# Output projection of a hybrid encoder on 16-bit halves, scaled by per-row powers of two

## The chip, the cores and the metric

The kernel runs on one core of a Trainium2 chip. The metric is the device time of one execution in microseconds (us). Before the change it is 2007.9 us, the median of three runs.

## The reference

One layer of an encoder is applied to two sequences that share weights: a prompt of 1024 rows and a sample of 4096 rows, each row 1024 wide, all in 32-bit floating point.

```python
def hybrid_layer(x, norm_g, w_in, sink, dw_w, dw_b, ln_g, ln_b, w_out):
    h = rms_norm(x, norm_g)
    proj = h @ w_in                       # 1024 -> 2816
    q, k, v, g_attn, u_conv, g_conv = jnp.split(proj, SPLITS, axis=-1)
    attn = windowed_gqa(q, k, v, sink)    # 8 heads of 64, 2 kv heads, |t-s| <= 128
    conv = conformer_conv(u_conv, dw_w, dw_b, ln_g, ln_b)   # GLU, 31 taps, LayerNorm, SiLU
    mix = jnp.concatenate([attn * silu(g_attn), conv * silu(g_conv)], axis=-1)
    return x + mix @ w_out                # 1024 -> 1024
...
y = rms_norm(hybrid_layer(x, ...), final_g)
```

The inputs' gains are scaled up (the LayerNorm's gain and bias by some 35 times, the first norm's gain by 6.8), so the two halves of `mix` reach far beyond what a 16-bit number holds unscaled.

## The kernel before, in words

The 5120 rows make ten groups of 512 rows (two of the prompt, eight of the sample), each of four blocks of 128 rows. A 32-bit operand enters a matmul as two parts, a high one (the value rounded) and a low one (what the rounding left), and a product is three matmuls: high by high, high by low, low by high. The input projection does this with 16-bit parts (`inproj`, L345: 8 slices of 128 rows times 3 pairs, 24 matmuls of 128x128 by 128x512 for each of 22 column tiles). The output projection does it with parts in the 32-bit rounded type (`out_mm`, L763: 8 slices times 3 pairs times 2 halves of 512 columns, 48 matmuls for a block, 1920 in all).

**Stage A** (to about 848 us) goes over the groups with `slot`: attention of one block, preparation of rows of the group after next (`prep_x`: load into a tile `xb`, norm, split, transposition by DMA) and a share of the next group's projection onto k, v, q and the attention gate. After each of the first six groups it also prepares two weight tiles for stage B (`split_late`: load into `xb`, `scale_w` finds a power of two from the largest entry by a reduction on DVE, a transposition and a broadcast on PE, and the parts go back to DRAM; L325 is its subtraction on POOL). At the end of `attention` three instructions form the gated output and its parts (L531 to L533: product on DVE, rounding on ACT, difference on DVE) in the tile `mx`, and a DMA stores the pair in DRAM (`md`, 512 KB).

**Stage B** goes over the groups again. `start_b` loads the group's prepared rows, `glu` projects eight column tiles (L632 on ACT, L633 on DVE free the matmul bank), `gates` projects four more through `conv_gate` (L639, SiLU on ACT into `sgc`, which the trace calls `x` after its tag). `conv_chunk` does the 31 taps on DVE (L695, L697), `ln_batch` and `ln_norm` the LayerNorm, and `ln_act` applies SiLU and gate (L751, L753) and splits into the tile `mc` (L754 on ACT, L755 on DVE). For each block `out_first` loads the rows `x` into `xb` and the attention pair into `ma`, and does the first 24 matmuls; `out_second` does the other 24 with `mc`, adds to the rows (L794 on DVE, two halves), sums the squares (L795 on ACT, writing back into the matmul's bank), finds the norm's factor on POOL in 11 small steps (L797, L260 to L269), scales (L806 on ACT), multiplies by `final_g` (L807 on POOL) and stores. Before the first block `load_out` brings in w_out with `split_wout`: a load into `xb`, for the four attention slices a factor (L335, POOL) and a scaling (L336, ACT), then rounding (L337, ACT) and difference (L338, POOL).

**What sets the order.** Nothing is issued as it is written down. Each operation is put into a plan with its engine and a cost in ns (`pl.op`), and `flush` simulates the engines and writes out every engine's instructions in the order of the simulated starts; of those that could start at the same time the one written first goes first. So a changed cost can change the order of everything near it. Tiles with a tag come from a ring of a fixed number (`xb` 2, matmul banks `mm` 4, `ma` 1, `mc` 2, `xn` 2), handed out in the order in which the code asks. All DMAs go through the queue of SP in the planned order; one that waits for its tile holds up those behind it. There are two flushes, one for each stage.

## Time and profile before

| | |
|---|---|
| runs | 2006.31, 2007.9, 2014.75 us; median 2007.9 |
| the profiled execution | 2009.39 us, its span 2007.5 us |
| mean granted TensorE clock | 0.975 of full speed |
| instructions | 25966 |

The profile is of one execution. Its span runs from the first to the last instruction; the execution is 1.9 us longer. PE is TensorE's matmuls, PEld its weight loads, DVE VectorE, ACT ScalarE, POOL GpSimd, SP SyncE, which only issues DMAs here. A matmul's duration is modelled and overlaps the next one's, so the rate of matmuls is read from the time of a run of them, not from their mean. A row names the line, engine, operation, out<-in and the number of instructions, then busy time, mean ns of one, and the idle time before them with what ended it. "x" before a number counts instructions. In the chain of waits each piece is followed back to what released it.

### The profile page before, as it was taken

The page shows a single profiled execution, that of the slowest core. Times are in us where ns is not written, and L with a number is a line of the kernel's source. Part 1 is how long each engine was busy: PE and PEld are TensorE (multiplying, and loading weights), DVE is VectorE, ACT ScalarE, POOL GpSimd, SP SyncE. Part 2 cuts the span into 40 slices and gives each one's busy share as a digit, 9 for nine tenths or more (in the row PEclk, how much of TensorE's full clock was granted, in tenths as well). Part 3 has the DMA queues.
Part 4 walks back from the last instruction along what each step waited for, and adds up shares of the span by engine and source line. Part 5 has one row for each costly group of instructions (what it writes and reads, how often), then busy time and mean ns, then how long its engine had stood idle before and what let it go on. Part 6 is the DMA issues. An engine that isn't in the chain of part 4 may idle for free. (4 is left out here: it accounts for less than half of the span.)

```text
span 2007.5 us, 25966 instructions
## 1 busy us (share of the span) xinstructions
PE 1868.7 (93%) x8953; PEld 1028.1 (51%) x8953; DVE 1800.7 (90%) x3703; ACT 907.0 (45%) x1962; POOL 663.1 (33%) x902
## 2 busy tenths in 40 slices
PE   3999998999999999987999899999999999999987
PEld 1444443444444444433648455564755657474675
DVE  7687897998998798699999998999999897998996
ACT  3577797797888777631213221221312222131332
POOL 1422233232333000060705508073451606143264
PEclk9999998999999999998999999999999999999988
DMA  7577978998999988641103211121221212132022
GB/s 246 137 151 195 232 188 214 223 201 222 226 206 235 232 215 175 141 147 63 64 21 127 74 53 63 73 74 43 84 84 64 86 73 74 42 105 95 32 95 95
DMA packets 364068, 259.39 MB, mean 129 GB/s; under 512 B 328352, under 2 KB 328480, under 8 KB 361376
## 3 DMA queue, kind: packets, MB, share of 16 engines
q1 hardware_dynamic: 363936, 257.73, 48.1%
q8 instruction: 70, 1.15, 0.2%
q14 instruction: 62, 0.51, 0.1%
HBM read 106.70 MB, written 69.21 MB: 88 GB/s over the span
## 5 line engine op out<-in xcount | busy, mean ns | idle before, releaser
L345 PE MATMUL mm<-x,wA 128*128 128x512 f16 x4800 | 1092.8, 383 | 32.3 <-ACT mm L795 17.4
L697 DVE SCALAR_TENSOR_TENSOR acc<-h,taps,acc 128x512 f32<-128x512 f32 (+2 forms) x1380 | 873.5, 693 | 2.0
L345 PEld LDWEIGHTS <-wA 128*128 128x128 f16 x4800 | 471.5, 99 | 583.6 <-issue 50.9
L763 PE MATMUL mm<-wo,mc 128*128 128x512 f32 x960 | 235.9, 401 | 4.0 <-ACT mc L754 3.9
L763 PE MATMUL mm<-wo,ma 128*128 128x512 f32 x888 | 218.9, 401 | 3.0 <-ACT mm L795 3.0
L493 DVE CUSTOM_DVE_ANT_0 pe<-s,dist_sb,sink_sb 128x384 f32<-128x384 f32 (+1 forms) x320 | 201.2, 658 | 15.1 <-PE s L490 13.3
L509 DVE SCALAR_TENSOR_TENSOR pe<-pe,rc 128x384 f16<-128x384 f32 (+1 forms) x320 | 187.9, 627 | 21.5 <-ACT pe L508 20.4
L763 PEld LDWEIGHTS mm<-wo,mc 128*128 128x128 f32 x960 | 179.9, 190 | 46.8 <-ACT mc L754 4.4
L797 POOL TENSOR_SCALAR v<-ms 128x1 f32<-128x1 f32 x38 | 34.3, 902 | 497.8 <-ACT mm L795 495.4
L763 PEld LDWEIGHTS mm<-wo,ma 128*128 128x128 f32 x888 | 167.8, 190 | 45.3 <-ACT mm L795 3.7
L501 ACT ACTIVATE pe<-pe,nm 128x384 f32<-128x384 f32 (+1 forms) x320 | 188.5, 590 | 3.2 <-DVE nm L493 2.8
L508 ACT ACTIVATE pe<-pe,rc 128x384 f16<-128x384 f32 (+1 forms) x320 | 175.6, 594 | 31.6 <-DVE rc L505 22.6
L807 POOL TENSOR_TENSOR xb<-xb,fg 128x1024 f32<-128x1024 f32 x37 | 129.9, 3511 | 88.7 <-ACT xb L806 88.6
L632 ACT ACTIVATE h<-mm,ucolh 128x512 f32<-128x512 f32 x40 | 27.3, 683 | 218.4 <-PE mm L345 218.4
L345 PE MATMUL mm<-x,xt 128*128 128x512 f16 x480 | 113.4, 395 | 0.0
L806 ACT ACTIVATE xb<-xb,r 128x1024 f32<-128x1024 f32 x37 | 42.4, 1145 | 151.9 <-POOL r L269 151.9
L489 PE MATMUL s<-kst,qst 128*128 128x384 f16 (+1 forms) x320 | 102.1, 321 | 8.9 <-DVE nm L493 6.6
L751 ACT ACTIVATE xn<-c,vec_sb 128x128 f32<-128x128 f32 x160 | 60.1, 456 | 108.6 <-PE c L744 85.7
L490 PE MATMUL s<-kst,qst 128*128 128x384 f16 (+1 forms) x320 | 101.7, 320 | 0.0
L795 ACT ACTIVATE mm<-xb 128x512 f32<-128x512 f32 x70 | 41.2, 589 | 120.5 <-DVE xb L794 120.5
L365 POOL TENSOR_SCALAR msv<-ms 128x1 f32<-128x1 f32 x36 | 8.4, 232 | 240.6 <-ACT xt L364 240.2
L267 POOL TENSOR_SCALAR rs_oa<-rs_oy,v 128x1 f32<-128x1 f32 x76 | 82.0, 1080 | 8.0
(164 smaller groups left out, 1940.0 us busy)
## 6 DMA issues: line engine op xcount, KB each, us to landing
xb<-x_s SPq DMA_DIRECT2D x62, 512.0 KB, 4.1
xd<-x SPq DMA_DIRECT2D x10, 2048.0 KB, 7.5
md<-mx SPq DMA_DIRECT2D x40, 512.0 KB, 3.4
x<-xd SPq DMA_DIRECT2D x10, 2048.0 KB, 7.9
ma<-md SPq DMA_DIRECT2D x37, 512.0 KB, 3.3
y_s<-xb SPq DMA_DIRECT2D x29, 512.0 KB, 2.6
xb<-x_p SPq DMA_DIRECT2D x14, 512.0 KB, 3.4
xb<-w_in SPq DMA_DIRECT2D x12, 512.0 KB, 4.6
```

Source lines behind the costliest of these rows:

```text
L267: pl.op(eng, cost + 80, lambda: en.tensor_scalar(a.t, view(cur), view(cur), v.t, ALU.mult, ALU.mult), [cur, v], [a])
L345: T.matmul(ps.t, w16.t[:, a, k, :], x16.t[:, b, k, :], start=(k == 0 and i == 0), stop=(k == KD - 1 and i == 2))
L489: T.matmul(sv(), q, kst.t[:, 2 * kv, kc0 : kc0 + n], start=True, stop=False)
L490: T.matmul(sv(), q, kst.t[:, 2 * kv + 1, kc0 : kc0 + n], start=False, stop=True)
L493: pl.op("DVE", 198 + n / 0.96, lambda: V.tensor_tensor_reduce(sc_(hh), sv(), dist_b.t[:, kv, d0 : d0 + n], gcol[:, hh : hh + 1], sink_sb[: ...
L501: pl.op("ACT", 280 + 0.834 * n, lambda hh=hh: S.activation(sc_(hh), sc_(hh), AF.Exp, bias=nm.t[:, hh : hh + 1], scale=-1.0, accum_out=den. ...
L508: pl.op("ACT", c_act(n, 1), lambda hh=hh: S.activation(p16(hh, 0), sc_(hh), AF.Copy, scale=rc.t[:, hh : hh + 1]), [rc, (pe, hh + 2)], [(pe ...
L509: pl.op("DVE", c_dve(n, 1), lambda hh=hh: V.scalar_tensor_tensor(p16(hh, 1), sc_(hh), rc.t[:, hh : hh + 1], p16(hh, 0), ALU.mult, ALU.subt ...
L697: pl.op("DVE", c_dve(n, 1), lambda: V.scalar_tensor_tensor(a.t[:, :n], src(), w, a.t[:, :n], ALU.mult, ALU.add), hr + [a], [a])
L751: pl.op("ACT", c_act(128, 2), lambda: S.activation(z.t[:, j, :], bk.t[:, j, :], AF.Silu, bias=vec_sb[:, 2, j : j + 1], scale=vec_sb[:, 1, ...
L763: T.matmul(po[hf].t, m.t[:, a, k - k0, :], wo.t[:, k, b, hf * 512 : (hf + 1) * 512], start=(k == 0 and a == 0 and b == 0), stop=(k == KD - ...
L807: pl.op("POOL", 2700, lambda: GP.tensor_tensor(xb.t, xb.t, fg.t, ALU.mult), [xb, fg], [xb])
```

## The change

The output projection's operands become 16-bit. Each of the 1024 rows of w_out (that is, each channel of `mix`) is multiplied by a power of two, its counterpart on the other side by the inverse, and the sum is scaled back by one common factor.

- `row_scales`, new, after group 6 of stage A: ten small DVE instructions that bound each channel of the convolution half by LayerNorm gain, bias and gate scale (`LNMAX`), take the power of two above it, and give `rsc` (factors for the rows of w_out) and `gsc` (inverse factors for the gates). For the attention half the factor is the one that `split_wout` computed before, with a constant `MSCALE` on the other side.
- `max_wout`, new, four slices after group 6 and four after group 7: loads a slice of w_out into `xb` and reduces it to its largest entry per row on DVE.
- `scale_wout`, new, after group 7: the common power of two, by the pattern of `scale_w` (nine small DVE instructions, a transposition and a broadcast on PE).
- `split_wout`: the factor of POOL goes away; two ACT passes (scale into 16 bit; scale in place) and POOL's difference for all eight slices.
- `attention`: the product has a tile `t2` of its own; the rounding scales by `MSCALE`; the difference is a scalar-tensor-tensor; the stored pair has 256 KB.
- `conv_gate`: a second ACT pass scales the gate by `gsc`, in place.
- `out_mm`: planned at 432 ns for a pair of matmuls, was 466; the matmuls are the same in number and shape.
- `out_second`: the add multiplies the matmul's result by the common factor `inv` (scalar-tensor-tensor).
- `wo`, `ma`, `mc` take half the bytes.

The diff, without the ten lines of `row_scales` and the nine small instructions of `scale_wout`:

```diff
@@ row_scales, max_wout, scale_wout (new) @@
+    def max_wout(k):
+        w = pl.buf(pxA, [P, D], F32, "xb", 2)
+        dma(lambda: w.t, lambda: w_out[:, k, :], 524288, [], [w])
+        pl.op("DVE", 1130, lambda: V.tensor_reduce(wmx_b.t[:, k : k + 1], w.t, AX.X, ALU.max, apply_absolute_value=True), [w], [(wmx_b, k)])
+    def scale_wout():
...
+        pl.op("PE", 110, lambda: T.transpose(pt.t[0:1, 0, :], mr.t[:, 0:1], ident), [mr], [pt])
...
+        pl.op("PE", 230, lambda: T.matmul(pb.t[:, 0, 0:2], ones, e2.t, start=True, stop=True), [e2], [pb])
...
@@ split_wout @@
-        if k < 4:
-            sc = small(smB, 1, "wsc", 2)
-            pl.op("POOL", 340, lambda: GP.tensor_scalar(sc.t, ...), ...)
-            pl.op("ACT", c_act(1024, 1), lambda: S.activation(w.t, w.t, AF.Copy, scale=sc.t), [w, sc], [w])
-        pl.op("ACT", c_act(1024), lambda: S.activation(wo.t[:, k, 0], w.t, AF.Copy), [w], [(wo, k)])
-        pl.op("POOL", 2200, lambda: GP.tensor_tensor(wo.t[:, k, 1], w.t, wo.t[:, k, 0].bitcast(F32), ALU.subtract), [w, (wo, k)], [(wo, k)])
+        sc = lambda: rsc_b.t[:, k : k + 1]
+        pl.op("ACT", c_act(1024, 1), lambda: S.activation(wo.t[:, k, 0], w.t, AF.Copy, scale=sc()), [w, rsc_b], [(wo, k)])
+        pl.op("ACT", c_act(1024, 1), lambda: S.activation(w.t, w.t, AF.Copy, scale=sc()), [w, rsc_b], [w])
+        pl.op("POOL", 2200, lambda: GP.tensor_tensor(wo.t[:, k, 1], w.t, wo.t[:, k, 0], ALU.subtract), [w, (wo, k)], [(wo, k)])
@@ attention @@
-        mx = pl.buf(pat, [P, 2, 4, P], F32R, "mx", 1)
+        t2, mx = pl.buf(pat, [P, 4, P], F32, "t2", 1), pl.buf(pat, [P, 2, 4, P], F16, "mx", 1)
...
+        pl.op("ACT", c_act(512), lambda: S.activation(mx.t[:, 0], t2.t, AF.Copy, scale=MSCALE), [t2], [(mx, 0)])
+        pl.op("DVE", c_dve(512, 1), lambda: V.scalar_tensor_tensor(mx.t[:, 1], t2.t, MSCALE, mx.t[:, 0], ALU.mult, ALU.subtract), [t2, (mx, 0)], [(mx, 1)])
+        md = dbuf([P, 1024], F16, f"md{si}_{ab}")
+        dma(lambda: md.t, lambda: mx.t.rearrange("p a j t -> p (a j t)"), 262144, [mx], [md])
@@ the loop over groups in stage A @@
+        else:
+            if gi == 6:
+                row_scales()
+            for k in range(4 * (gi - 6), min(KD, 4 * (gi - 6) + 4)):
+                max_wout(k)
+            if gi == 7:
+                scale_wout()
@@ conv_gate @@
+        pl.op("ACT", c_act(512, 1), lambda: S.activation(sgc.t[:, i, j, :], sgc.t[:, i, j, :], AF.Copy, scale=gsc_b.t[:, j : j + 1]), [(sgc, (i, j)), gsc_b], [(sgc, (i, j))])
@@ wo, ln_act, out_first: F32R becomes F16; the load of ma has 262144 bytes @@
@@ out_mm @@
-                pl.op("PE", 466, mm, [(m, a) if k0 else m, (wo, k)], po)
+                pl.op("PE", 432, mm, [(m, a) if k0 else m, (wo, k)], po)
@@ out_second @@
-                pl.op("DVE", c_dve(512), lambda: V.tensor_tensor(xs(), xs(), po[hf].t, ALU.add), [po[hf], (xb, hf)], [(xb, hf)])
+                pl.op("DVE", c_dve(512, 1), lambda: V.scalar_tensor_tensor(xs(), po[hf].t, inv_b.t, xs(), ALU.mult, ALU.add), [po[hf], (xb, hf), inv_b], [(xb, hf)])
```

## Rows read from the trace of the kernel before

**Rows 1.** The page's busy time, share of the span and instructions of each engine

```profile
PE 1868.7 (93%) x8953; PEld 1028.1 (51%) x8953; DVE 1800.7 (90%) x3703; ACT 907.0 (45%) x1962; POOL 663.1 (33%) x902
```

**Rows 2.** Busy time by stretch; columns us, busy (x instructions), PEclk, DMA share, GB/s

```profile
600.00:800.00 200.00, 198.87 (x1066) 93.30 (x1064) 171.09 (x448) 154.56 (x376) 19.12 (x55) 1.00 0.92 213
848.00:943.00 95.00, 74.04 (x325) 33.55 (x324) 95.00 (x155) 19.61 (x22) 31.78 (x11) 0.89 0.28 95
943.00:1200.00 257.00, 240.89 (x1080) 147.72 (x1079) 254.36 (x511) 60.97 (x120) 93.43 (x96) 0.96 0.22 76
...
1290.00:1409.60 119.60, 113.02 (x514) 67.97 (x512) 118.13 (x185) 26.58 (x53) 53.37 (x48) 0.97 0.20 71
1409.60:1525.00 115.40, 111.16 (x514) 67.84 (x512) 109.28 (x173) 26.80 (x53) 48.45 (x48) 0.99 0.20 73
1525.00:1640.00 115.00, 113.00 (x514) 67.98 (x513) 104.60 (x165) 26.70 (x53) 41.41 (x48) 0.98 0.21 74
...
1924.00:2007.50 83.50, 66.95 (x277) 52.87 (x277) 67.54 (x207) 27.56 (x59) 41.58 (x60) 0.88 0.26 95
```

**Rows 3.** The chain that ended last: shares by line, then start us, us, what

```profile
by line: DVE acc L697 13.6%; PE mm L763 12.4%; PE mm L345 3.2%; POOL xb L807 1.1%; DVE wA L697 1.1%; DVE bst L712 0.8%; DVE h L633 0.7%; issue 0.7%; PE c L744 0.7%; DVE xb L794 0.5%; DVE acc L695 0.4%; POOL rs_oa L267 0.4%; DMA ma<-md 0.3%;
...
1215.26 16.17 POOL xb L807
...
1539.98 11.20 PE mm L763 x48
...
1580.03 10.39 PE mm L345 x48
```

**Rows 4.** Matmul groups by line; columns as on the page (busy us, mean ns, idle)

```profile
L345 PE MATMUL mm<-x,wA 128*128 128x512 f16 x4800 | 1092.8, 383 | 32.3 <-ACT mm L795 17.4 <-DMA x<-xd 7.9 <-DMA x<-pT 3.0
...
L763 PE MATMUL mm<-wo,mc 128*128 128x512 f32 x960 | 235.9, 401 | 4.0 <-ACT mc L754 3.9
```

**Rows 5.** Groups of DVE, by line

```profile
L794 DVE TENSOR_TENSOR xb<-xb,mm 128x512 f32<-128x512 f32 x76 | 48.6, 681 | 25.1 <-DMA xb<-x_s 24.8 <-issue 0.3
...
L633 DVE SCALAR_TENSOR_TENSOR h<-h,mm 128x512 f32<-128x512 f32 x40 | 27.1, 678 | 13.5 <-ACT h L632 13.5
...
L290 DVE TENSOR_REDUCE w_mx<-xb 128x1 f32<-128x1024 f32 x12 | 14.5, 1208 | 0.0
...
L316 DVE SCALAR_TENSOR_TENSOR wA<-qst,w_sg,wA 128x1024 f16<-128x1024 f32 x3 | 3.8, 1276 | 0.0
...
L283 DVE TENSOR_TENSOR pe<-pe,ng 128x1024 f32<-128x1024 f32 x3 | 3.6, 1216 | 0.0
...
L307 DVE TENSOR_SCALAR w_sg<-s 128x1 f32<-128x1 f32 x19 | 2.9, 154 | 12.6 <-PE s L305 12.3
```

**Rows 6.** Groups of POOL and ACT by line, then DVE's timeline from 849 to 890 us

```profile
L639 ACT ACTIVATE x<-mm,ucol 128x512 f32<-128x512 f32 x40 | 25.9, 683 | 64.5 <-PE mm L345 64.5
L325 POOL TENSOR_TENSOR xt<-xb,xt 128x1024 f16<-128x1024 f32 x12 | 25.5, 2128 | 87.7 <-ACT xt L324 87.7
...
L338 POOL TENSOR_TENSOR wo<-xb,wo 128x1024 fp32r<-128x1024 f32 x8 | 19.5, 2447 | 7.5 <-ACT wo L337 7.5
...
849.26 25.49 DVE L697 SCALAR_TENSOR_TENSOR acc<-h,taps,acc 128x384 f32<-128x384 f32 x48
...
875.26 14.61 DVE L697 SCALAR_TENSOR_TENSOR acc<-h,taps,acc 128x384 f32<-128x384 f32 x12
```

**Rows 7.** DMA issues; KB each, median us from issue to landing

```profile
y_s<-xb SPq DMA_DIRECT2D x29, 512.0 KB, 2.6
...
y_s<-xb SPq DMA_DIRECT2D x2, 256.0 KB, 2.0
```

**Rows 8.** Waits of DVE, PE and SP's queue: us in total, times, longest us

```profile
DVE xb L794 <- DMA xb<-x_s: 24.8, 4, 8.3
...
PE s L305 <- DVE w_e L303: 19.1, 6, 10.8
...
SPq L229 <- POOL xt L325: 31.7, 9, 6.3
```

51 lines of the change are left out of this document (39 added, 12 removed).

## The prediction

> **What bounds the kernel now.** I read the busy shares first: TensorE (PE) 93%, VectorE (DVE) 90%, ScalarE (ACT) 45%, GpSimd (POOL) 33% [rows 1]. Two engines near the top say that the share alone won't decide, so the next view is the table by stretch [rows 2]. The change puts its new work into stage A (attention, up to about 848 us) and takes work out of stage B (convolution and output projection, from there to the end). Three regimes are to be seen there. From 600 to 800 us PE is busy 198.9 of 200 us and DVE 171.1: PE is the limit and DVE has 28.9 us free. From 848 to 1200 us DVE is busy 95.0 of 95 and 254.4 of 257 us: DVE is the limit. The step from 1290 to 1409.6 us is still nearly so (DVE idle 1.5 us, PE 6.6). In the group steps from 1409.6 us on PE is the limit: from 1525 to 1640 us PE is idle 2.0 of 115 us and DVE 10.4. The last 83.5 us are a tail in which neither is full.
>
> Then the chain of waits, whose first long piece starts at 1215 us [rows 3]. It goes to and fro between DVE's convolution (L697) and PE, and the output matmuls (L763) stand on it with 12.4% of the span, 249 us. This is the number that the forecast rests on: matmuls elsewhere lie beside something longer.
>
> **The change part by part.** *Matmuls.* All 1920 output matmuls go from 32-bit rounded to 16-bit operands of the same shape, 128x128 by 128x512; the number stays. The mean durations (401 and 383 ns) [rows 4] overlap and give no rate, so I take it from chain pieces: 48 matmuls of L763 take 11.20 us, 233.3 ns each, and 48 of the 16-bit L345 take 10.39 us, 216.5 ns each [rows 3]. So PE gets 16.8 ns less per matmul, 32.3 us over all 1920. On the chain the 249 us are 1067 matmuls; at 216.5 ns they save 17.9 us. The other 853 lie before 1215 us, where DVE is full, or beside the chain, and I give them nothing. Ends: 0 (DVE or another wait takes it all) and 32.3 us. I take **-17.9**. The cover for it: in a PE-bound step 192 matmuls lose 3.2 us, and DVE has 6.1 us idle in the step from 1409.6 us and 10.4 in that from 1525 us [rows 2]; next late is DVE.
>
> A rule speaks against this term. The Trainium skill (Perfetto Trace Analysis, Identifying the Most-Contended Engine) calls matmul busy time a poor measure of headroom and wants the used share of its peak rate and the busy share of the weight loads instead. The weight loads are busy 68.0 of 115 us in the step from 1525 us [rows 2], so by the rule PE has some 40% to spare and a shorter matmul would save nothing. The chain pieces of back-to-back matmuls decide for me, since there every 48 of them take their 11.20 us.
>
> *DVE, residual add (L794).* Two instructions for each of 40 blocks become a scalar-tensor-tensor with a per-row scalar (76 stand in the row; those of two late blocks write a tile of another name). Lower end 0: such an instruction with a constant, reading PSUM, takes 678 ns (L633) beside 681 for the add now. Upper end: at 1024 columns with a per-row scalar it takes 1276 ns (L316) against 1216 (L283), so 60 ns each, 4.8 us [rows 5]. I take half the upper end, **+2.4**, since DVE is the limit for about half of stage B.
>
> *Preparing the weights.* POOL loses four one-column instructions, and its eight subtractions write 16-bit: 2447 ns (L338) become 2128 (L325, the same shape with 16-bit output), 2.6 us less. POOL is not the limit, but DVE runs slowly beside it: 48 taps took 25.49 us, 0.53 each, and 12 of the same size soon after, beside L338 by the order of the code, 14.61, 1.22 each [rows 6]. DVE is full there, so I count **-2.0**, ends 0 and -2.6. ACT does sixteen 1024-wide passes in place of twelve, each at most twice the 0.68 us of the 512-wide L639, so 5.5 us more; from 848 to 943 us ACT is busy 19.6 of 95 us [rows 2], so nothing. If that cover were gone, 5.5.
>
> *Gate scaling.* 40 more ACT passes of 512 columns, each at most the 683 ns of L639 [rows 6], 27 us; 36 of them in stage B, where ACT is busy 26.7 of 115 us. Behind each on ACT's queue wait the next gate, and the tanh that frees PE's bank; four matmul banks cover 0.7 us. Nothing; uncovered it is 0.7 on each of nine steps, 6 us.
>
> *Pairs through memory.* Store and load of the attention half shrink from 512 to 256 KB. The landing of an output goes from 2.6 to 2.0 us at these sizes [rows 7]. The loads stand on the chain with 0.3% (6 us) [rows 3] in two pieces, so **-1.2**; ends 0 and -6, were they to leave it. Forty stores get as much shorter in stage A, beside PE: nothing. The product, its copy and its residual in stage A stay three instructions of the same sizes.
>
> *Bounds of w_out.* New in stage A: eight loads of 512 KB, eight DVE reductions of 1024 columns at 1208 ns (L290), 19 small DVE instructions at about 154 (L307) [rows 5], 12.6 us in all; one transposition and one broadcast on PE that wait for DVE in the middle; placed by the code behind groups 6 and 7 of ten, which I put between 600 and 800 us. DVE's 28.9 free us from 600 to 800 cover them [rows 2]. What may show is the wait in PE's queue: such broadcasts cost 19.1 us in 6 waits, 3.2 each [rows 8], and PE's next projection stands behind them. I take one, **+3.0**; ends 0 and 12.6.
>
> *The order.* The plan gets 432 ns per pair of matmuls in place of 466, sees the new instructions and smaller tiles, and writes out another order. No row shows what that does; ends -5 and +5, the size of the gaps between neighbouring steps' lengths (119.6 and 115.4 us) [rows 2]. I take 0, as it can fall either way.
>
> Sum: -17.9 + 2.4 - 2.0 - 1.2 + 3.0 = -15.7 us. The profiled execution took 2009.4 us (span 2007.5), 1.5 above the median of 2007.9; I set the sum against the median: 1992.2, **1992**.
>
> **The rivals.** *DVE or the x tiles take it over:* with PE quicker, the blocks of a burst come faster, and each needs one of two x tiles that must first be stored and loaded again; DVE already waits 24.8 us in four places for that load [rows 8]. Against it: DVE's idle time in three later steps exceeds 3.2 us. Were only the tail's matmuls (about 190, 3.2 us) and a little more saved, 6 in all, the time is 2007.9 - 6 + 2.2 (the other terms) = 2004.
>
> *All of PE's time comes out,* also before 1215 us, as the plan may shift DVE work into PE's shade: 2007.9 - 32.3 + 2.2 = 1978. Against: DVE has only 2.6 us idle from 943 to 1200 us [rows 2].
>
> *The matmuls save nothing,* because PE has room, or because the new pairs still run at 233 ns: the other terms alone, 2007.9 + 2.2 = 2010. The first reading is that of the rule of the Trainium skill above. Against: 16-bit matmuls of this shape run at 216.5 ns in the same stretch.
>
> *Slower: the bound on w_out blocks the queue of SP.* Its eight loads take x tiles that the next group's rows also need; each can hold SP, with the attention's transpositions behind it, as the weight tiles' stores and loads behind L325 do now, 31.7 us in nine waits, 3.5 each [rows 8]. Eight of these are 28 us, and with DVE's 12.6 uncovered 40.6 in place of the 3.0: 2030. It decides once 29 of those us show. Against: the reductions free a tile in 1.2 us, and nothing else hangs on them until stage B.
>
> **How the numbers follow.** A measurement here can tell about 0.5%, so faster means below 1997.9 and slower above 2017.9. Chances: the forecast 0.55, all of PE's time 0.13 (together faster, 0.68); DVE or the tiles 0.20, nothing saved 0.05 (no change, 0.25); the blocked queue 0.07. The range 1976 to 2006 holds the forecast with its unknowns (-5 to +5 for the order, 2.4 either way for L794, up to 9.6 more for stage A), the full gain and the take-over, some 0.83 together, as its lower end cuts the full gain where the order falls well; it leaves out the blocked queue and the case of nothing saved.
>
> **What would show it.** Chain pieces of 48 output matmuls at 10.4 us instead of 11.2; steps from 1409.6 us on shorter by about 3 us, those before 1200 us unchanged or longer by half a microsecond each; DVE's idle time there down to some 7 us; stage A ending within 3 us of where it does; ACT up by some 30 us, with no engine waiting for the gates. It is wrong if the steps of stage B keep their length while PE goes idle, if the output matmuls keep 233 ns, or if stage A ends over 10 us later or earlier.

## The result: slower, and the profile after

The changed kernel took 2036.5 us (median of four runs, 2017.7 to 2041.9) against 2011.3 for the kernel before on the same chip (2006.3 to 2017.5): a ratio of 1.010 on record, interval 1.0062 to 1.0137 (of the medians alone it would be 1.013). The forecast was 1992 and faster. The profiled one of these executions was the quickest of the four, so the rows below come from a repeat of the same kernel: 2035.9 us, ratio 1.0152 (1.0133 to 1.017), its profiled execution 2039.0 us with a span of 2037.2.

Line numbers move: the projection L345 is now L387, the output matmuls L763 L812, the taps L697 L746, the residual add L794 L843, the sum of squares L795 L844, the norm's first POOL step L797 L846, the scaling L806 L855, the gain's product L807 L856.

The busy shares of the repeat, for [rows 1]:

```profile
PE 1843.6 (90%) x8956; PEld 855.7 (42%) x8956; DVE 1788.4 (88%) x3730; ACT 941.2 (46%) x2008; POOL 746.8 (37%) x898
```

PE, DVE and the weight loads all lost share. ACT gained the 34 us of its new passes, and POOL gained 84 us of busy time although the change takes work from it. No engine has become the limit. Something waits.

The table by stretch of the repeat, for [rows 2] (us, then busy of PE, PEld, DVE, ACT, POOL, PEclk, DMA share, GB/s); the last three are three steps of stage B from the first convolution instruction of one group to that of the next, and stand for the steps from 1409.6 us on before:

```profile
600.00:800.00 200.00, 197.23 (x1049) 92.44 (x1048) 173.02 (x448) 148.15 (x365) 16.05 (x44) 1.00 0.89 211
848.00:943.00 95.00, 73.35 (x327) 33.60 (x327) 92.72 (x158) 28.04 (x31) 39.09 (x10) 0.87 0.29 96
943.00:1200.00 257.00, 230.94 (x1077) 107.32 (x1075) 244.94 (x504) 66.71 (x130) 115.71 (x96) 0.96 0.18 65
...
1389.20:1499.20 110.00, 97.17 (x450) 45.10 (x449) 97.88 (x165) 26.96 (x54) 55.65 (x45) 0.94 0.16 58
1499.20:1615.10 115.90, 103.68 (x484) 48.34 (x483) 101.92 (x167) 28.99 (x57) 51.01 (x40) 0.96 0.16 55
1615.10:1732.20 117.10, 111.84 (x520) 51.86 (x519) 102.86 (x165) 29.32 (x57) 50.43 (x50) 0.97 0.18 63
```

The steps are no shorter than before: from the first convolution instruction of one group to that of the next, the three before last 108.2, 116.1 and 114.0 us. And now both engines stand idle in them: from 1499.2 to 1615.1 us PE for 12.2 us and DVE for 14.0, where from 1525 to 1640 us before PE had 2.0 and DVE 10.4. From 943 to 1200 us DVE, which was full, has 12.1 us idle.

The chain of the repeat, its five longest pieces (start us, us, what), for [rows 3]:

```profile
1342.28 13.47 POOL xb L856
1467.22 14.04 POOL xb L856
1591.31 13.39 POOL xb L856
1845.36 13.15 PE mm L387 x48
1979.90 10.36 PE mm L812 x48
```

Two things are to be seen. Forty-eight output matmuls take 10.36 us, 215.8 ns each, as forecast: the faster rate is there. And the three longest pieces are single instructions of POOL, the gain's product on an x tile, whose usual time is 2.4 us. Followed on in time, one of them reads like this:

```profile
1465.99 1.16 ACT xb L855
1467.15 0.07 issue
1467.22 14.04 POOL xb L856
1481.28 2.63 DMA y_s<-xb
1483.93 0.03 issue
1483.96 3.23 DMA xb<-x_s
...
1487.31 1.41 DVE xb L843 x2
```

POOL's product ends 14 us after it began, then the tile is stored, then loaded again for the next block, and DVE's add has been waiting for that load. The waits of the repeat (total us, times, longest), for [rows 8] and the idle times of [rows 4, 5], say the same for the whole stage:

```profile
ACT xb L855 <- POOL r L275: 185.6, 26, 19.9
...
PE mm L387 <- ACT mm L844: 64.4, 11, 9.8
DVE xb L843 <- DMA xb<-x_s: 53.2, 7, 11.1
...
DVE xb L843 <- POOL xb L856: 11.5, 1, 11.5
```

The load of x cost DVE 24.8 us in four waits before; now 64.7 with the wait for POOL. PE's wait for a bank went from 17.4 to 64.4: DVE's add comes late, the squares behind it too, and they free the bank. PE pays once more behind such a wait: it stood idle for 8.9 us before 1488.87 us, and from 1488.8 to 1492 us its granted clock was 0.50 of full speed, the lower of its two levels (1.2 GHz). What this costs was not tried by itself.

Why does a 2.4 us instruction take 14? The timeline of the repeat around it (start us, us, engine and instruction, idle before):

```profile
1465.73 1.40 DVE L843 SCALAR_TENSOR_TENSOR xb<-mm,inv,xb 128x512 f32<-128x512 f32 x2
1467.05 12.00 DVE L746 SCALAR_TENSOR_TENSOR acc<-h,taps,acc 128x512 f32<-128x512 f32 x18
1467.22 14.03 POOL L856 TENSOR_TENSOR xb<-xb,fg 128x1024 f32<-128x1024 f32 x1 [1.26 <-ACT xb L855]
1481.28 0.34 SPq L231 DMA_DIRECT2D y_s<-xb  x1
```

Two of the new adds, then 18 taps end to end; POOL's product begins 0.17 us into the taps and ends only 2.2 us after the last of them. It is a pattern: six of these products in the repeat begin 0.09 to 0.18 us into a run of taps that directly follows the new add, and they take 13.5, 14.0, 13.4, 6.8, 7.4 and 7.4 us. (A seventh, of 8.8 us, begins in a run of taps behind L681.) One-column POOL instructions suffer too, one of them 15.52 us at 1211.08 us, whose like takes 0.19. The kernel before has such cases as well, behind its plain add: the product of 16.17 us of [rows 3], two more of 6.8 us, and one first step of the norm of 7.1. Its products over the whole run (min/median/max in ns):

```profile
L807 POOL TENSOR_TENSOR xb<-xb,fg x37: 2341/2761/16160, 975.2 to 1987.4; 128x1024 f32<-128x1024 f32 x37
```

So the change did not bring the long ones in; it made them many.

### The profile page after: what moved, and what is told of

Same layout as the page of the kernel before. It is cut to its first block, busy times and chain, and to the rows that moved or that the text cites. A ratio compares the mean times of both kernels' runs of the same rounds, so it can differ in the third digit from the quotient of the medians.

```text
span 2015.9 us, 26017 instructions
## 1 busy us (share of the span) xinstructions
PE 1835.9 (91%) x8956; PEld 855.2 (42%) x8956; DVE 1797.4 (89%) x3730; ACT 941.2 (47%) x2008; POOL 708.6 (35%) x898
## 4 chain that ended last, share of the span: by engine, by line
DVE 38%; PE 27%; POOL 8%; ACT 5%; issue 2%; DMA 2%; DVEq 0%; POOLq 0%; ACTq 0%; SPq 0%
DVE acc L746 26%; PE mm L387 15%; PE mm L812 7%; POOL xb L856 2%; POOL rs_ob L274 2%; PE o L566 2%; DVE xb L843 1%; ACT pe L543 1%; POOL v L846 1%; PE s L531 1%; DVE pe L535 1%; DVE wA L746 1%; DVE pe L551 1%; POOL rs_oa L273 1%; PE s L532 1%
## 5 line engine op out<-in xcount | busy, mean ns | idle before, releaser
L387 PE MATMUL mm<-x,wA 128*128 128x512 f16 x4800 | 1100.7, 384 | 74.9 <-ACT mm L844 48.3
L746 DVE SCALAR_TENSOR_TENSOR acc<-h,taps,acc 128x512 f32<-128x512 f32 (+2 forms) x1380 | 852.9, 679 | 1.4
L387 PEld LDWEIGHTS <-wA 128*128 128x128 f16 x4800 | 472.9, 99 | 631.0 <-issue 104.8
L846 POOL TENSOR_SCALAR v<-ms 128x1 f32<-128x1 f32 x38 | 70.6, 1859 | 480.6 <-ACT mm L844 478.2
L812 PE MATMUL mm<-wo,mc 128*128 128x512 f16 x960 | 215.8, 381 | 4.0 <-ACT mc L803 4.0
L812 PE MATMUL mm<-wo,ma 128*128 128x512 f16 x888 | 200.2, 381 | 8.1 <-ACT mm L844 4.9
L543 ACT ACTIVATE pe<-pe,nm 128x384 f32<-128x384 f32 (+1 forms) x320 | 188.5, 590 | 12.2 <-DVE nm L535 11.9
L856 POOL TENSOR_TENSOR xb<-xb,fg 128x1024 f32<-128x1024 f32 x37 | 129.4, 3497 | 71.3 <-ACT xb L855 71.0
L812 PEld LDWEIGHTS <-mc 128*128 128x128 f16 x960 | 94.1, 98 | 113.4 <-ACT mc L803 5.0
L812 PEld LDWEIGHTS <-ma 128*128 128x128 f16 x888 | 87.0, 98 | 113.2 <-issue 9.7
L844 ACT ACTIVATE mm<-xb 128x512 f32<-128x512 f32 x70 | 41.8, 597 | 156.6 <-DVE xb L843 156.6
L855 ACT ACTIVATE xb<-xb,r 128x1024 f32<-128x1024 f32 x37 | 42.4, 1145 | 155.3 <-POOL r L275 155.3
L387 PE MATMUL mm<-x,xt 128*128 128x512 f16 x480 | 111.4, 390 | 0.0
L843 DVE SCALAR_TENSOR_TENSOR xb<-mm,inv,xb 128x512 f32<-128x512 f32 x76 | 53.3, 741 | 45.8 <-DMA xb<-x_s 25.9
```

Of the source, the lines that this page charges most:

```text
L387: T.matmul(ps.t, w16.t[:, a, k, :], x16.t[:, b, k, :], start=(k == 0 and i == 0), stop=(k == KD - 1 and i == 2))
L543: pl.op("ACT", 280 + 0.834 * n, lambda hh=hh: S.activation(sc_(hh), sc_(hh), AF.Exp, bias=nm.t[:, hh : hh + 1], scale=-1.0, accum_out=den. ...
L746: pl.op("DVE", c_dve(n, 1), lambda: V.scalar_tensor_tensor(a.t[:, :n], src(), w, a.t[:, :n], ALU.mult, ALU.add), hr + [a], [a])
L812: T.matmul(po[hf].t, m.t[:, a, k - k0, :], wo.t[:, k, b, hf * 512 : (hf + 1) * 512], start=(k == 0 and a == 0 and b == 0), stop=(k == KD - ...
L843: pl.op("DVE", c_dve(512, 1), lambda: V.scalar_tensor_tensor(xs(), po[hf].t, inv_b.t, xs(), ALU.mult, ALU.add), [po[hf], (xb, hf), inv_b], ...
L846: pl.op(eng, 650 if en is GP else 140, lambda: en.tensor_scalar(v.t, ms.t[:, 0:1], ms.t[:, 1:2], EPS, ALU.add, ALU.add), [ms], [v])
```

## The experiments

They stand in the order in which they were run, but for the last two. "Planned price" is the cost that the planner gets for the residual add: 602 ns in the plain form, 663 with a per-row operand; it sets the order of instructions, not their duration. Several times came out beyond the band of the theory that they bear out (1975.0, 1976.4, 1982.5 below it, 1993.4, 2001.0 and 2040.8 a little above): the direction was forecast there, the size not quite. Where a run met no theory, the text says so.

**What the 16-bit operands alone give.** The repeat, and a version without the rest of the change (no gate pass, plain add, no bounds; the row factors are 1):

> The changed kernel once more, so that the other three have it on the same chip. Every theory: 2017 to 2042 us, as in its four runs so far; steps of stage B of 116 to 118 us, TensorE waiting 40 to 60 us for banks of matmul results that ScalarE's squares free (17 us before the change).

```diff
...
-        pl.op("ACT", c_act(512, 1), lambda: S.activation(sgc.t[:, i, j, :], sgc.t[:, i, j, :], AF.Copy, scale=gsc_b.t[:, j : j + 1]), [(sgc, (i, j)), gsc_b], [(sgc, (i, j))])
...
-                pl.op("DVE", c_dve(512, 1), lambda: V.scalar_tensor_tensor(xs(), po[hf].t, inv_b.t, xs(), ALU.mult, ALU.add), [po[hf], (xb, hf), inv_b], [(xb, hf)])
+                pl.op("DVE", c_dve(512), lambda: V.tensor_tensor(xs(), xs(), po[hf].t, ALU.add), [po[hf], (xb, hf)], [(xb, hf)])
```

> Leaves out the bounds of w_out in stage A, the second pass over the gates and the common factor in the residual add (the factors are all set to one), so the 16-bit pairs are left alone. Theory A (the quicker matmuls run into the return of the banks: square on ScalarE, queued behind the norm's factor on GpSimd): time as the changed kernel within 10 us, 2010 to 2035, TensorE still waiting over 35 us for the squares. Theory B (the added instructions eat the gain): 1985 to 1998 us, clearly below the kernel before, waits for the squares back to 20 us.

Measured: the repeat 2035.9 as above; the reduced version 1975.0, ratio 0.9845 (0.982 to 0.987). So the 16-bit operands, with the smaller pairs and tiles and the order that come with them, are worth some 31 us, and the rest of the change costs twice that. Not all of the 31 is the matmuls' rate: stage A ends 8 us earlier in this run, as its first convolution instruction shows, before the change and here:

```profile
848.48 0.86 DVE L695 TENSOR_SCALAR acc<-h,taps,vec_sb 128x384 f32<-128x384 f32 x2
```

```profile
840.72 0.86 DVE L740 TENSOR_SCALAR acc<-h,taps,vec_sb 128x384 f32<-128x384 f32 x2
```

**The planned price of the matmuls and the release of the banks.** One run puts the price of a pair back to 466 ns; another lets the squares write a scratch tile, so that the add and not ACT frees the bank.

```diff
-                pl.op("PE", 432, mm, [(m, a) if k0 else m, (wo, k)], po)
+                pl.op("PE", 466, mm, [(m, a) if k0 else m, (wo, k)], po)
```

> The changed kernel with the planned cost of a pair of output matmuls put back from 432 to 466 ns; the instructions are the same, their order may differ. Theory C (the new order of the plan is what costs): 1990 to 2003 us. Theory A: within 10 us of the changed kernel, since the instructions that free a bank stay the same.

```diff
-                sq = spare(4, [P, 512], F16) if gi == NG - 1 else po[hf]
+                sq = spare(4, [P, 512], F16) if gi == NG - 1 else pl.buf(pb, [P, 512], F16, "sqs", 2)
```

> The changed kernel with the squares' unused output written to a scratch tile in SBUF instead of back into the bank; the bank is then free after the two passes that read it on VectorE (the add), no longer after ScalarE's square. Theory A: TensorE's wait for squares (48 us in the changed kernel's profile) goes, and 15 to 30 us of the time with it: 1990 to 2010 us. Theories B and C: no change beyond 5 us, 2017 to 2042.

Measured: 2048.8, ratio 1.0221 (1.0206 to 1.0236), and 2037.6, ratio 1.016 (1.0143 to 1.0177). The old price makes it 13 us worse, so the order matters by more than the 5 us I allowed it, and the theory that the new order is what costs falls. The bank theory falls too: the time is the same, as PE's wait only moves from the squares (64.4 us) to the add itself (74.3).

**Each added part taken away.** Without the gate pass (the gates stay unscaled); with the plain add at its plain price (the common factor is left out); without the bounds (the factors are 1); and with four x tiles of their own in stage B in place of the two.

```diff
-        pl.op("ACT", c_act(512, 1), lambda: S.activation(sgc.t[:, i, j, :], sgc.t[:, i, j, :], AF.Copy, scale=gsc_b.t[:, j : j + 1]), [(sgc, (i, j)), gsc_b], [(sgc, (i, j))])
```

> The changed kernel without ScalarE's second pass over the gates (40 passes of 721 ns); the convolution half then lacks its row factors. The three additions that the kernel with 16-bit pairs alone leaves out are put to the test one by one; together they cost some 60 us (2036 against 1975). Theory G (the pass costs through ScalarE's queue, in front of the squares and the tanh): 1995 to 2015 us. Theory D (the residual add in its new form on VectorE is what costs) and theory S (the bounds in stage A): within 8 us of the changed kernel, 2028 to 2044.

```diff
-                pl.op("DVE", c_dve(512, 1), lambda: V.scalar_tensor_tensor(xs(), po[hf].t, inv_b.t, xs(), ALU.mult, ALU.add), [po[hf], (xb, hf), inv_b], [(xb, hf)])
+                pl.op("DVE", c_dve(512), lambda: V.tensor_tensor(xs(), xs(), po[hf].t, ALU.add), [po[hf], (xb, hf)], [(xb, hf)])
```

> The changed kernel with the residual add put back to a plain two-operand add (the common factor is left out). Theory D: 1990 to 2010 us, steps of stage B back to 108 to 111 us. Its direct price is only 80 times 64 ns, 5 us (745 against 681 ns), so more than 10 us would mean that the new form holds up something else, GpSimd's steps or the return of the x tiles. Theories G and S: 2026 to 2040 us.

```diff
+    V.memset(rsc_b.t, 1.0)
+    V.memset(gsc_b.t, 1.0)
+    V.memset(inv_b.t, 1.0)
+    V.memset(wmx_b.t, 1.0)
...
-        else:
-            if gi == 6:
-                row_scales()
-            for k in range(4 * (gi - 6), min(KD, 4 * (gi - 6) + 4)):
-                max_wout(k)
-            if gi == 7:
-                scale_wout()
```

> The changed kernel without the bounds of w_out in stage A (no extra loads, reductions and small instructions; all factors set to one). Theory S: stage A ends 8 to 11 us earlier (840.7 us in the kernel with the pairs alone, 851.6 now) and the time falls by 8 to 15 us, 2020 to 2030. Theories G and D: the rest of the 60 us stays, so not below 2015.

```diff
-        xb = spare(qb, [P, D], F32) if tail and qb > 0 else pl.buf(pxA, [P, D], F32, "xb", 2)
+        xb = spare(qb, [P, D], F32) if tail and qb > 0 else pl.buf(pb, [P, D], F32, "xo", 4)
```

> The changed kernel with four tiles of their own for the rows x of stage B, in the SBUF that the smaller weights free, instead of the ring of two. Theory X (the additions lengthen the round of an x tile: load, add, square, factor, scale, multiply, store; VectorE waits 53 us for the load at the end of it): these waits go and the time falls to 1975 to 2000 us, below the kernel before. Theories G and D in their direct form (their own time on the engines): within 10 us of the changed kernel, 2026 to 2045.

Measured: gate pass away 2035.4, ratio 1.0122 (1.0088 to 1.0156); plain add 1992.2, 0.9914 (0.9884 to 0.9944); bounds away 2029.3, 1.0101 (1.0067 to 1.0135); four tiles 2001.0, 0.9958 (0.9939 to 0.9977). The gate pass is hidden within the noise. The bounds cost some 10 us (the two intervals just touch), and these lie in stage A: the first convolution instruction starts at 851.58 us with them (the repeat) and at 840.48 without:

```profile
851.58 0.86 DVE L744 TENSOR_SCALAR acc<-h,taps,vec_sb 128x384 f32<-128x384 f32 x2
```

```profile
840.48 0.86 DVE L741 TENSOR_SCALAR acc<-h,taps,vec_sb 128x384 f32<-128x384 f32 x2
```

The one edit that turns the result around is the form of the 80 adds, an instruction that became 64 ns longer. More x tiles take away most of the loss, which agrees with the chain: the tiles come back late.

**Form or order?** The plain add also came with another planned price. So the two were crossed: plain add at the price of 663, whose order is that of the changed kernel on every engine (the common factor is left out), and the new add at 602, whose order is that of the run with the plain add.

```diff
-                pl.op("DVE", c_dve(512, 1), lambda: V.scalar_tensor_tensor(xs(), po[hf].t, inv_b.t, xs(), ALU.mult, ALU.add), [po[hf], (xb, hf), inv_b], [(xb, hf)])
+                pl.op("DVE", c_dve(512, 1), lambda: V.tensor_tensor(xs(), xs(), po[hf].t, ALU.add), [po[hf], (xb, hf)], [(xb, hf)])
```

> The residual add as a plain two-operand add (common factor left out), but planned at the new form's 663 ns: every engine's order is that of the changed kernel, only the form of 80 instructions on VectorE differs. Theory O (the 61 ns in the plan move the adds and all after them, and that order costs the 44 us between 2036 and 1992): 2025 to 2040 us, steps of stage B of 116 to 117 us. Theory F (the new form itself, with PSUM first, a row factor and x, costs them on the chip, directly or through GpSimd): 1987 to 2000 us.

```diff
-                pl.op("DVE", c_dve(512, 1), lambda: V.scalar_tensor_tensor(xs(), po[hf].t, inv_b.t, xs(), ALU.mult, ALU.add), [po[hf], (xb, hf), inv_b], [(xb, hf)])
+                pl.op("DVE", c_dve(512), lambda: V.scalar_tensor_tensor(xs(), po[hf].t, inv_b.t, xs(), ALU.mult, ALU.add), [po[hf], (xb, hf), inv_b], [(xb, hf)])
```

> The other corner: the new form of the add, planned at the plain add's 602 ns, so that every engine's order is that of the kernel with the plain add (1992 us). Nothing is left out. Theory O: 1990 to 2002 us, below the kernel before (5 us at most for the longer instructions). Theory F: 2025 to 2040 us.

Measured: 1976.4, ratio 0.9831 (0.9796 to 0.9867), and 2040.8, ratio 1.015 (1.0118 to 1.0181). In either order the new form is the slow one. In the changed kernel's order it costs 1.0152 / 0.9831, 3.3% or some 65 us, and in the other 1.015 / 0.9914, 2.4% or some 48; 80 times 64 ns is 5.1 of these. The products of POOL with the plain add in the changed kernel's order (min/median/max in ns; the repeat's stand further below):

```profile
L856 POOL TENSOR_TENSOR xb<-xb,fg x37: 2340/2652/6175, 976.0 to 1957.4; 128x1024 f32<-128x1024 f32 x37
```

**The factor on the other operand.** The row multiplied by the inverse factor and added to the matmul's result, with the norm's epsilon scaled to match and nothing left out; alone, then with four tiles:

```diff
-        pl.op("DVE", 105, lambda: V.tensor_scalar(inv_b.t, pb.t[:, 0, 0:1], 2.0 ** -14, None, ALU.mult), [pb], [inv_b])
+        pl.op("DVE", 105, lambda: V.tensor_scalar(isg_b.t, pb.t[:, 0, 1:2], 2.0 ** 13, None, ALU.mult), [pb], [isg_b])
+        pl.op("DVE", 105, lambda: V.tensor_scalar(eps_b.t, isg_b.t, isg_b.t, EPS, ALU.mult, ALU.mult), [isg_b], [eps_b])
...
-                pl.op("DVE", c_dve(512, 1), lambda: V.scalar_tensor_tensor(xs(), po[hf].t, inv_b.t, xs(), ALU.mult, ALU.add), [po[hf], (xb, hf), inv_b], [(xb, hf)])
+                pl.op("DVE", c_dve(512), lambda: V.scalar_tensor_tensor(xs(), xs(), isg_b.t, po[hf].t, ALU.mult, ALU.add), [po[hf], (xb, hf), isg_b], [(xb, hf)])
...
-        pl.op(eng, 650 if en is GP else 140, lambda: en.tensor_scalar(v.t, ms.t[:, 0:1], ms.t[:, 1:2], EPS, ALU.add, ALU.add), [ms], [v])
+        pl.op(eng, 650 if en is GP else 140, lambda: en.tensor_scalar(v.t, ms.t[:, 0:1], ms.t[:, 1:2], eps_b.t, ALU.add, ALU.add), [ms, eps_b], [v])
```

> The same sum scaled the other way: x times the inverse of the common factor plus the matmul's result, with the norm's epsilon scaled to match, so SBUF comes first and PSUM second as in the plain add; planned at 602 ns. Nothing is left out. Theory O: 1990 to 2002 us, like the run with the new form planned at 602. Theory F, if it hangs on the operands' places: 1987 to 1997 here and 2025 or more there; if on the row factor: 2025 or more in both.

```diff
-        xb = spare(qb, [P, D], F32) if tail and qb > 0 else pl.buf(pxA, [P, D], F32, "xb", 2)
+        xb = spare(qb, [P, D], F32) if tail and qb > 0 else pl.buf(pb, [P, D], F32, "xo", 4)
```

> The run before with four x tiles of their own in stage B (worth 35 us on the changed kernel, 2036 to 2001). Theory O with theory X: with a good order little waits for x tiles (13 us in the kernel with the pairs alone), so 1975 to 1995 us; no more than 15 us below the same without them.

Measured: 2046.0, ratio 1.0178 (1.0147 to 1.0209), and 2012.4, ratio 1.0012 (0.9996 to 1.0028). No better: it isn't the matmul's result going through the multiplier. The second was set down at 1975 to 1995 for the theory that the order does it, which these two and the crossing before them refute.

**What of the new form does it?** Four runs. ACT multiplies x by the inverse factor after its load, the add is plain, nothing is left out:

```diff
+        pl.op("ACT", c_act(1024, 1), lambda: S.activation(xb.t, xb.t, AF.Copy, scale=isg_b.t), [xb, isg_b], [xb])
...
-                pl.op("DVE", c_dve(512, 1), lambda: V.scalar_tensor_tensor(xs(), po[hf].t, inv_b.t, xs(), ALU.mult, ALU.add), [po[hf], (xb, hf), inv_b], [(xb, hf)])
+                pl.op("DVE", c_dve(512, 1), lambda: V.tensor_tensor(xs(), xs(), po[hf].t, ALU.add), [po[hf], (xb, hf)], [(xb, hf)])
```

> x is multiplied by the inverse of the common factor on ACT after its load (one pass of 1024 columns for each block, about 1.1 us of ACT), eps is scaled to match, and the 80 adds are the plain two-operand form of the kernel before; nothing is left out. Theory (the form of the 80 adds is what makes the changed kernel slow): near the run with the plain add and the planned price of 663, 1976, plus what 40 passes on ACT cost where they are not hidden, 0 to 15: 1976 to 1992, ratio 0.983 to 0.992. Rival (the common factor itself costs it, wherever it is applied): 2010 or more.

A constant in place of the per-row factor, same order:

```diff
-                pl.op("DVE", c_dve(512, 1), lambda: V.scalar_tensor_tensor(xs(), po[hf].t, inv_b.t, xs(), ALU.mult, ALU.add), [po[hf], (xb, hf), inv_b], [(xb, hf)])
+                pl.op("DVE", c_dve(512, 1), lambda: V.scalar_tensor_tensor(xs(), po[hf].t, 1.0, xs(), ALU.mult, ALU.add), [po[hf], (xb, hf)], [(xb, hf)])
```

> The common factor is left out: the 80 adds stay scalar-tensor-tensor but multiply by the constant 1.0 in place of the per-row factor; order as in the changed kernel on every engine. Theory A (the operation itself does it): 2025 to 2045, as the changed kernel. Theory B (reading the per-row factor does it): 1975 to 1990, as the plain add with this order.

A one-column plain add directly behind each new add; and the reverse, a one-column scalar-tensor-tensor with the per-row factor behind each plain add. Apart from these the order is that of the changed kernel; `tn_b` is a scratch tile of one column:

```diff
-                pl.op("DVE", c_dve(512, 1), lambda: V.scalar_tensor_tensor(xs(), po[hf].t, inv_b.t, xs(), ALU.mult, ALU.add), [po[hf], (xb, hf), inv_b], [(xb, hf)])
+                pl.op("DVE", c_dve(512, 1), lambda: (V.scalar_tensor_tensor(xs(), po[hf].t, inv_b.t, xs(), ALU.mult, ALU.add), V.tensor_tensor(tn_b.t, xs()[:, 0:1], po[hf].t[:, 0:1], ALU.add)), [po[hf], (xb, hf), inv_b], [(xb, hf)])
```

> The changed kernel with a one-column plain tensor-tensor add right behind each of the 80 new adds, nothing left out; order otherwise as in the changed kernel. Theory C (it matters what the tap runs directly follow, and a plain add ahead of them lets POOL in): 1980 to 2000. Theory D (what the large add is made of matters, not what stands directly ahead of the taps): 2035 to 2055, the changed kernel plus 80 small instructions of 0.1 us.

```diff
+                pl.op("DVE", c_dve(512, 1), lambda: (V.tensor_tensor(xs(), xs(), po[hf].t, ALU.add), V.scalar_tensor_tensor(tn_b.t, po[hf].t[:, 0:1], inv_b.t, xs()[:, 0:1], ALU.mult, ALU.add)), [po[hf], (xb, hf), inv_b], [(xb, hf)])
```

> The common factor is left out of the result: the 80 adds are the plain form, each followed by a one-column scalar-tensor-tensor with the per-row factor that writes a scratch column; order otherwise as in the changed kernel. Theory C (what stands directly ahead of the taps decides): 2020 to 2050, slow again though the large add is the plain one. Theory D: 1976 to 1992.

Measured, in this order: 2015.4, ratio 1.0006 (0.9986 to 1.0026); 1993.4, 0.9913 (0.9888 to 0.9939); 1992.1, 0.9911 (0.9891 to 0.993); 1990.7, 0.9904 (0.9882 to 0.9926). The first came out where its rival put it (2010 or more), yet it doesn't settle the matter: ACT now stands in its queue until the load of x lands, with its other work behind it, and POOL's first step of the norm took 2355 ns in the mean where the run with the plain add in the changed kernel's order has 1072 (waits of that run, then a group of it):

```profile
ACT xb L830 <- DMA xb<-x_s: 53.0, 14, 7.2
```

```profile
L849 POOL TENSOR_SCALAR v<-ms,epst 128x1 f32<-128x1 f32 x38 | 89.5, 2355 | 460.5 <-ACT mm L847 459.2 <-ACT wA L847 1.2
```

So scaling x instead has a price of its own, and a plain add doesn't keep POOL free in every order. (The norm's first step also reads the scaled epsilon there; whether that matters was not tried.)

The constant takes some 48 us off (1.0152 to 0.9913). The add reads the same tile and bank and goes from 745 ns to 686, close to the plain form's 681 (that run's durations, min/median/max):

```profile
L843 DVE SCALAR_TENSOR_TENSOR xb<-mm,xb x76: 675/686/736, 956.7 to 1968.5; 128x512 f32<-128x512 f32 x76
```

So most of it takes the per-row operand, or the 59 ns by which the add is longer with it; no run parts the two. Only most, as the norm's first step on POOL still took 6.4 us four times in that run and 8.9 and 9.5 us once each. And it takes the add standing directly ahead of the taps: with a one-column instruction of 155 ns in between, the whole changed kernel with nothing left out is as much faster (0.9911). The reverse run fails the theory's other half, that whatever stands directly ahead of the taps decides: a small instruction with the per-row factor there did no harm.

The traces say the same by count. Of POOL's instructions from 945 us on, without the eight subtractions for w_out, these took over 5 us: 21 in the repeat, 177 us together, 20 of them begun in the first microsecond of a run of taps behind the new add; 8 (58 us) with the constant; 2 (12 us) with the plain add in the same order; none with either one-column instruction. In other orders the plain add has them too: 5 (43 us) in the kernel before, 13 (96 us) where ACT scales x. Nor does the moment explain it. The norm's first step begins 0.94 to 0.95 us into such a run eleven times in the repeat and eleven times with the plain add in the same order: seven took 5.8 to 6.5 us in the one, and nine took 1.2 us and one 5.3 in the other. Its durations in the repeat, then with the plain add:

```profile
L846 POOL TENSOR_SCALAR v<-ms x38: 289/402/7835, 959.9 to 2007.3; 128x1 f32<-128x1 f32 x38
```

```profile
L846 POOL TENSOR_SCALAR v<-ms x38: 302/734/5335, 959.9 to 1941.1; 128x1 f32<-128x1 f32 x38
```

**The smallest form of the remedy.** The instruction in between need not read anything: a one-column memset behind each add, same order, nothing left out. And the one-column add with four x tiles:

```diff
+                pl.op("DVE", c_dve(512, 1), lambda: (V.scalar_tensor_tensor(xs(), po[hf].t, inv_b.t, xs(), ALU.mult, ALU.add), V.memset(tn_b.t, 0.0)), [po[hf], (xb, hf), inv_b], [(xb, hf)])
```

> As the run with a one-column plain add behind each of the 80 new adds, but the small instruction is a one-column memset that reads nothing; nothing left out, order the same on every engine. If any instruction between the add and the taps lets POOL in: 1985 to 1995. If it has to be one that reads the bank and the tile: 2030 to 2050, as the changed kernel.

```diff
-        xb = spare(qb, [P, D], F32) if tail and qb > 0 else pl.buf(pxA, [P, D], F32, "xb", 2)
+        xb = spare(qb, [P, D], F32) if tail and qb > 0 else pl.buf(pb, [P, D], F32, "xo", 4)
...
+                pl.op("DVE", c_dve(512, 1), lambda: (V.scalar_tensor_tensor(xs(), po[hf].t, inv_b.t, xs(), ALU.mult, ALU.add), V.tensor_tensor(tn_b.t, xs()[:, 0:1], po[hf].t[:, 0:1], ALU.add)), [po[hf], (xb, hf), inv_b], [(xb, hf)])
```

> The changed kernel with a one-column plain add behind each of the 80 new adds and four own x tiles in stage B; nothing left out. The run with the one-column add alone took 1992.1, that with four tiles alone 2001.0. If both act on the same wait (x tiles that come back late because POOL is held out): 1985 to 1992, little below the first alone. If they act on different waits: 1970 to 1982.

Measured: the memset 1982.5, ratio 0.989 (0.9868 to 0.9912); the four tiles with the one-column add 2007.5, ratio 1.0011 (0.9998 to 1.0023). **The memset version computes what the changed kernel computes and beats both kernels**, by 21 us the kernel before and by some 53 the changed one, at 59 ns a piece:

```profile
L843 DVE MEMSET tn<- x80: 59/59/59, 959.1 to 1971.4; 128x1 f32 x80
```

Its timeline at the place that answers to the one shown above for the repeat:

```profile
1439.17 1.41 DVE L843 SCALAR_TENSOR_TENSOR xb<-mm,inv,xb 128x512 f32<-128x512 f32 x2
1439.86 0.06 DVE L843 MEMSET tn<- 128x1 f32 x1
1440.51 0.74 DVE L746 SCALAR_TENSOR_TENSOR acc<-h,taps,acc 128x512 f32<-128x512 f32 x1
1440.53 0.06 DVE L843 MEMSET tn<- 128x1 f32 x1
1440.58 2.89 POOL L856 TENSOR_TENSOR xb<-xb,fg 128x1024 f32<-128x1024 f32 x1 [1.26 <-ACT xb L855]
1441.18 2.85 DVE L746 SCALAR_TENSOR_TENSOR acc<-h,taps,acc 128x512 f32<-128x512 f32 x1
...
1443.49 0.34 SPq L231 DMA_DIRECT2D y_s<-xb  x1
```

The order of issue is add, memset, add, memset, taps (the rows go by recorded start, and the last memset's lies 0.02 us behind the tap's). The same product of POOL, begun as closely behind the add, ends after 2.89 us in the middle of the taps, and this time it is DVE that waits: the tap beside it takes 2.85 us in place of some 0.7. DVE pays for this, as the 1380 main taps of stage B take 869.9 us here and 839.8 in the repeat, and the kernel is still 53 us faster, as the x tile is on its way 11 us sooner here. Over the whole run its durations (min/median/max), first in the repeat, then with the memset:

```profile
L856 POOL TENSOR_TENSOR xb<-xb,fg x37: 2337/2358/14028, 989.4 to 2015.4; 128x1024 f32<-128x1024 f32 x37
```

```profile
L856 POOL TENSOR_TENSOR xb<-xb,fg x37: 2341/2595/4602, 975.6 to 1958.9; 128x1024 f32<-128x1024 f32 x37
```

The median even rises; the few long ones are gone, and three of them were the longest pieces of the chain. No POOL instruction but the subtractions for w_out takes over 5 us any more. The steps that answer to those shown first, in the memset version:

```profile
1365.30:1468.50 103.20, 97.00 (x452) 45.21 (x451) 103.20 (x172) 26.92 (x54) 50.00 (x45) 0.97 0.17 62
1468.50:1574.20 105.70, 102.34 (x482) 47.89 (x481) 104.05 (x175) 29.28 (x57) 42.74 (x40) 0.99 0.17 60
1574.20:1687.60 113.40, 109.71 (x515) 51.15 (x514) 106.04 (x174) 29.84 (x57) 46.84 (x59) 0.98 0.19 70
```

DVE idles 0, 1.7 and 7.4 us in them instead of 12.1, 14.0 and 14.2. With four tiles the small instruction makes no gain (0.9958 without it, 1.0011 with it, and its 80 times 155 ns are 12.4 us of DVE). This fits both acting on the same wait, the late tile, but 2007.5 lies above both bands that were set down (1985 to 1992 and 1970 to 1982), so it isn't shown; two products still took 5.1 and 10.6 us there. Why four tiles then stay 1% behind the one-column add with two was not found; the order of the work differs there.

## Why the prediction was wrong, step by step

**Residual add, the step that failed.** The text had "+2.4", with 0 and 4.8 as ends, from the difference of durations alone. The duration was nearly right: 745 ns against 681, 5.1 us over 80 instead of at most 4.8. The cost was 65 us against the plain form in the same order, over thirteen times the upper end. What the runs showed in its place is a wait: POOL's instructions beside the taps behind the new add are held up, the x tiles come back late, and DVE's adds and PE's banks with them. I priced the instruction on its own engine and never asked what it does to another engine that runs beside it. A row of mine pointed that way: the piece of 16.17 us for POOL's product at 1215 us [rows 3], seven times its usual time. I read the chain for its matmuls and took that piece as a curiosity; it was the thing that the change made many of. The rival nearest to what happened was that of the x tiles, with DVE's 24.8 us of waiting for their loads; its place was right (64.7 us now), but I let faster matmuls cause it, and gave it 2004.

**Matmuls: rate and place right, size a little small.** 216 ns instead of 233 came true (48 in 10.36 us). I let only the 1067 matmuls on the chain count, -17.9. As a whole the version with 16-bit operands alone gained 31 us, and the changed kernel with the plain add in the same order 34 (ratio 0.9831, 27 to 41). That looks like the rival "all of PE's time comes out": my sum with all of PE's 32.3 in place of the 17.9, and without the add's 2.4, would be -32.5. Place by place it isn't so. In the 556.6 us from 1367.6 to 1924.2 us before, where PE is the limit, stand 960 output matmuls, worth 16.1 us at 16.8 ns each; by the same convolution instructions this stretch lasts 537.4 us with 16-bit operands alone and 533.2 with the plain add, 19 and 23 us less. The other 960 gave little: all of stage B outside that stretch got 4.4 and 8.1 us shorter, and the rest of the 31 is stage A's 8. So the term had its place right and came out somewhat larger. How much of the surplus is the order, a price alone having moved the time by up to 16 us, was not tried.

**The weight loads' rule.** The Trainium skill (Perfetto Trace Analysis, Identifying the Most-Contended Engine) judges TensorE's headroom by the used share of its peak rate and the busy share of the weight loads; I took the second alone. As the weight loads were busy 59% of a step, I read it as room in PE, so that a faster matmul would save nothing, and gave that rival 5%. The runs speak against this reading: with weight loads that short of full, the steps where PE is the limit became 19 to 23 us shorter. The used share of the peak was not worked out.

**Bounds of w_out.** +3.0 taken, ends 0 and 12.6; without them stage A ended 11 us earlier and the time was 10 us lower by the ratios. So they cost about 10, near the upper end: DVE's idle time in stage A did not cover them. That stage A ended 3.1 us later than before, just as I had said, is luck: stage A gained some 8 us elsewhere (848.5 us before, 840.5 without the bounds), where I had written "nothing" for the smaller pairs and tiles. Which of these parts gave the 8 us was not tried.

**POOL's share of the weights.** The forecast of 2128 ns per subtraction was far off: in the repeat it takes 4712 (all eight, beside the taps).

```profile
L380 POOL TENSOR_TENSOR wo<-xb,wo 128x1024 f16<-128x1024 f32 x8 | 37.6, 4712 | 21.6 <-ACT xb L379 21.6
```

It lies off the chain, and its cost doesn't show: from 848 to 943 us DVE had 158 instructions, where it had 155 before. The -2.0 was not tested by itself.

**Gate scaling.** 0, as forecast: without it 2035.4, ratio 1.0122 against 1.0152, intervals that overlap. ACT rose by 34 us, as it should.

**The order.** 0 taken, ends -5 and 5. Two runs with one edit each and another planned price lay 13 us (466 for 432) and 16 us (602 for 663, plain add) from their counterparts; a third, 602 for 663 with the new add, changed nothing (ratios 1.015 and 1.0152). In a kernel whose order is computed from prices, an unknown order can be worth three times what I allowed.

**The slower rival.** SP's queue blocked by the loads of w_out, 0.07: not seen. The bounds' whole cost is 10 us, in place of the 40.6 of that rival. That its 2030 lies near the result is luck: the time went that way by another path.

So the other parts together make a kernel of 1976, and the one term that I put at 2.4 us turned the sign of the whole. My own sign of being wrong, steps of stage B that keep their length while PE goes idle, is what the profile showed. The memset version stands 0.6%, some 12 us, above the plain add in the same order (0.989 to 0.9831): 80 adds at 65 ns more (741 against 676) and 80 memsets of 59 ns are 9.9 us of DVE.

## What to carry to other kernels

When an edit changes an instruction's operands, look at what runs beside it on the other engines and not at its duration alone: a one-column memset put between a DVE add with a per-row operand and a long run of DVE instructions took 53 us off here. In a profile, look for single instructions with a maximum several times their median, and for whether the chain goes through them; a mean hides them. And before an expected gain is trusted to a computed order, cross the edit with the old and new price, as a price alone moved the time by 13 and by 16 us here, and once not at all.

## What was not expected of the hardware

A POOL instruction that begins just behind a DVE add, ahead of a run of DVE taps, can stay unfinished through the whole run: 14.03 us in place of 2.34 for the product, 15.52 in place of 0.19 for a one-column tensor-scalar. In the changed kernel's order it took three things together to have many of these: the per-row operand or the length it brings (with a constant the time is 1993), the full-width instruction (a one-column one with the same operand, behind the plain add, gave 1991), and no other instruction between it and the taps (with a memset of 59 ns 1983). In other orders the plain add did it too, most of all with the 16.17 us before the change.

The Trainium skill (SBUF — State Buffer, the sections SBUF: two separate sides and Who interferes with whom) says that VectorE and GpSimd share one pair of SBUF ports, that a VectorE instruction with two SBUF inputs contends for it with a GpSimd instruction that reads SBUF, and that whichever starts first has the pair for its whole instruction. The taps are such instructions and POOL's are such readers. In the memset version the trace agrees: one tap stretched to 2.85 us beside a POOL product of 2.89. In the changed kernel a wait of POOL for one such instruction would be some 0.7 us, and 18 taps pass; what happens between two taps that follow each other closely, the sections don't say. That the new add counts as a second reader of SBUF through its factor, so that no gap is left for POOL between the taps ahead and those behind, would fit the constant and the memset. Against it stand the long waits behind the plain add, and the runs of taps behind another DVE instruction with two SBUF inputs (L804): in the repeat a one-column POOL instruction took at most 1.9 us there, and a product 4.1. So this is argued, not shown. What the chip does there stays open.
